# First-layer queries and keys in six weight tiles instead of eight, the gates' input columns as separate fp32 products

## The chip, the cores and the metric

The kernel runs on one core of one Trainium2 chip. The metric is the time of one launch on the device, in microseconds; the median of three runs is shown, and one further execution was recorded by the hardware profiler. PE (TensorE) multiplies, DVE (VectorE) and ACT (ScalarE) work on tiles, POOL (GpSimd) does a little elementwise work, and SP (SyncE) issues most of the DMAs.

## The reference, cut to what matters

One step of a two-layer decoder over 1024 prompt tokens and 8 sample tokens (1032 columns in all), width 1024. Only the first layer's input projection is touched:

```python
h = rmsnorm(x, norm_mix_pre[l])
q, k, v, r, glr, qm = split_cols(h @ w_in_a[a], IN_A_SIZES)   # 384, 384, 768, 768, 16, 256 columns
q = q.reshape(B, L, 4, 96) * (96 ** -0.5)
k = k.reshape(B, L, 4, 96)
g = jax.nn.log_sigmoid((glr @ w_gate_up[a] + b_gate[a]).astype(jnp.float32)) / 16
o, S = gla_recurrence(q, k, v, g, gla_state[a])               # gated linear attention, 4 heads
o_mem = mem_attend(qm, mem_k[l], mem_v[l])                    # attention into 256 memory tokens
```

`glr` are the 16 gate columns: a second, small product makes the 384 gates from them. The rest of the first layer (output projection, MLP) and the whole second layer are the same before and after.

## The kernel before, in words

Everything is kept transposed: features on the 128 partitions, tokens along the free axis, in three chunks of 384, 384 and 264 columns (`CH`). The 1024 input features are eight slices `k` of 128.

A large product is done in three passes of a reduced format: x and each weight are split into a rounded part and a remainder, x into `xh` and `xl`, a weight into `wh` and `wl`. `proj` (L241) multiplies one weight tile of 128 output columns with one chunk: for each of the eight slices `wh*xh`, `wh*xl`, `wl*xh`, 24 products that add up in one accumulator bank. A weight tile therefore costs 72 products over the three chunks. `wload` (L212) fetches a weight tile (512 KB), ACT rounds it to `wh` (L153), DVE makes `wl` (L154).

The norm's factor r is one number per token. It is not put on x but on the result: each accumulator is read out ("evicted") by DVE, which multiplies by r. r itself comes from squares on ACT, sums on DVE, a product with `ones` on PE (L199) and a few steps on ACT and DVE.

The first layer's stages are, in the order of the program:

1. `load_x` (L1003): 12 pieces of x, four for each chunk, two slices each, go through seven load buffers `ld` (L985). ACT rounds each piece with the norm's gain to `xh` (L994), DVE makes `xl` (L995), ACT squares it (L181). A buffer can be loaded again when all its readers are done.
2. `in_qm` (L1159): two weight tiles, the queries for the memory attention.
3. The keys and values of the memory (`memkv`), woven in between the first two query tiles.
4. The memory attention: scores into `sA` (L382), softmax on DVE and ACT, transposes (L401), output (L409), eight times; then the same for the 8 sample tokens, which ends with the transposes L461. In between stand the products of the other six query and key tiles, which keep PE busy while the softmax runs, and `gates` (L1228).
5. The branch (L1401): gated linear attention in one of two forms, chosen by a flag from the gates; behind it everything else.

Queries and keys stand in `qk`, eight slots of 128 partitions of which a head uses 96, rows 0 to 95. A weight tile is one head: 96 columns, or 112 for the first one, where the 16 gate columns stand behind the head's and land in rows 96 to 111 of slot 0. Row 112 is 1.0 for the bias. So `gates` multiplies rows 96 to 127 of slot 0 (32 rows) with the gate weights `wg`, 17 rows filled up with zeros.

The accumulators of stages 1 to 3 are two banks `mm` and four `mx` (`pm0`, L1207), taken in turn by `mmps`. Instructions are put in order, engine by engine, by a scheduler with priorities; `late` and `tick` (L122) hold a product back until so many columns of other products have been put ahead of it. On every engine the order is then fixed: an instruction that waits holds up those behind it.

## Time and profile before

| | |
|---|---|
| median of three runs | 2275.08 us (2273.16 to 2279.07) |
| profiled execution, time | 2279.71 us |
| its span, first to last instruction | 2277.9 us |
| mean granted TensorE clock | 0.99 |
| branch of the gated attention (start of the first L1303) | 222.29 us |
| first product on PE | 11.96 us |

A row of the timeline gives the start, the length, the engine, the line, the operation with its tiles, how many instructions are merged, and in brackets the idle time of the engine ahead of it and what ended it. Products overlap, so the distance between two starts, not the length, is what one costs. A fp32 product that is not split counts as two records.

### The profile page before, as it was taken

How to read it: one execution, taken by the hardware profiler on the slowest of the kernel's cores; microseconds unless marked ns; L12 is line 12 of the kernel's file. 1: busy time of each engine (PE TensorE's matmuls, PEld its weight loads, DVE VectorE, ACT ScalarE, POOL GpSimd, SP SyncE). 2: the span in 40 equal slices, each digit the busy share in tenths (PEclk: the TensorE clock that was granted, in tenths of full speed). 3: DMA queues.
4: the chain of work that ended last, by engine and by line, in shares of the span. 5: the costliest groups of instructions: out<-in, count | busy, mean ns of one | idle time of the engine just before them, and what ended most of it. 6: DMA issues, size and time to landing. Idle time of an engine off the chain costs nothing. (4 is left out here: it accounts for less than half of the span.)

```text
span 2277.9 us, 40266 instructions
## 1 busy us (share of the span) xinstructions
PE 2210.1 (97%) x16340; PEld 2093.2 (92%) x16340; DVE 1508.5 (66%) x2788; ACT 1062.4 (47%) x2064; POOL 76.0 (3%) x78
## 2 busy tenths in 40 slices
PE   7999999999999999899999999999999999999997
PEld 6868999899999999899999878679999999999996
DVE  7543565767887777756559555645987777756547
ACT  6451544546654544333334355644754445333333
POOL 0000100000000000320000000200000000000000
PEclk9999999999999999999999999999999999999998
DMA  5412013544363448665324200413364445735422
GB/s 197 144 53 98 13 55 94 158 144 130 123 202 131 139 153 305 234 243 165 108 62 148 94 20 29 133 61 101 114 198 161 154 138 212 261 106 160 152 95 75
DMA packets 136261, 305.41 MB, mean 134 GB/s; under 512 B 11274, under 2 KB 65619, under 8 KB 135779
## 3 DMA queue, kind: packets, MB, share of 16 engines
q1 hardware_dynamic: 122962, 276.75, 36.9%
q0 software_dynamic: 3312, 13.30, 1.9%
q10 hardware_dynamic: 9792, 12.68, 1.5%
q8 instruction: 131, 2.15, 0.4%
q14 instruction: 64, 0.52, 0.1%
HBM read 215.25 MB, written 89.51 MB: 134 GB/s over the span
## 5 line engine op out<-in xcount | busy, mean ns | idle before, releaser
L153 ACT CAST wh<-ws 128x512 fp32r<-128x512 f32 (+1 forms) x264 | 190.2, 728 | 353.4 <-DVE ws L576 104.5
L245 PE MATMUL mm<-xh,wh 128*128 128x384 f32 (+3 forms) x904 | 295.0, 327 | 15.3 <-ACT wh L153 12.0
L723 PE MATMUL mx<-xf,wh 128*128 128x258 f32 x1048 | 297.7, 284 | 0.0
L154 DVE TENSOR_TENSOR wl<-ws,wh 128x512 fp32r<-128x512 f32 (+1 forms) x264 | 216.4, 826 | 121.1 <-ACT wh L153 120.1
L724 PE MATMUL mx<-xf,wh 128*128 128x258 f32 x1048 | 296.0, 282 | 0.0
L725 PE MATMUL mx<-xf,wl 128*128 128x258 f32 x1048 | 295.1, 282 | 0.0
L247 PE MATMUL mm<-xh,wl 128*128 128x384 f32 (+3 forms) x904 | 292.9, 324 | 0.2 <-DVE wl L154 0.2
L246 PE MATMUL mm<-xl,wh 128*128 128x384 f32 (+3 forms) x904 | 292.3, 323 | 0.0
L153 ACT CAST wh<-wr 128x1024 fp32r<-128x1024 f32 x98 | 103.0, 1051 | 326.3 <-PE sx L889 307.3
L154 DVE TENSOR_TENSOR wl<-wr,wh 128x1024 fp32r<-128x1024 f32 x98 | 122.3, 1248 | 172.9 <-ACT wh L153 172.9
L889 PE MATMUL mx<-sa,wh 128*128 128x258 f32 x784 | 221.2, 282 | 6.1 <-DVE sa L154 6.1
L888 PE MATMUL mx<-sa,wh 128*128 128x258 f32 x784 | 222.3, 284 | 0.8 <-DVE aw L565 0.7
L890 PE MATMUL mx<-sa,wl 128*128 128x258 f32 x784 | 221.0, 282 | 0.0
L724 PEld LDWEIGHTS mx<-xf,wh 128*128 128x128 f32 x1048 | 198.0, 189 | 0.4
L723 PEld LDWEIGHTS mx<-xf,wh 128*128 128x128 f32 x1048 | 197.6, 189 | 0.4
L725 PEld LDWEIGHTS mx<-xf,wl 128*128 128x128 f32 x1048 | 197.9, 189 | 0.0
L245 PEld LDWEIGHTS mm<-xh,wh 128*128 128x128 f32 (+1 forms) x904 | 167.1, 185 | 25.6 <-ACT wh L153 12.5
L247 PEld LDWEIGHTS mm<-xh,wl 128*128 128x128 f32 (+1 forms) x904 | 166.7, 184 | 8.8 <-issue 6.5
L246 PEld LDWEIGHTS mm<-xl,wh 128*128 128x128 f32 (+1 forms) x904 | 167.2, 185 | 7.7 <-issue 5.8
L889 PEld LDWEIGHTS mx<-sa,wh 128*128 128x128 f32 x784 | 148.9, 190 | 6.3 <-DVE sa L154 6.3
L888 PEld LDWEIGHTS mx<-sa,wh 128*128 128x128 f32 x784 | 147.9, 189 | 1.9 <-DVE aw L565 1.1
L890 PEld LDWEIGHTS mx<-sa,wl 128*128 128x128 f32 x784 | 148.6, 189 | 0.0
(539 smaller groups left out, 5764.5 us busy)
## 6 DMA issues: line engine op xcount, KB each, us to landing
ra<-awd SPq DMA_DIRECT2D x98, 516.0 KB, 4.1
ws<-in_w_up SPq DMA_DIRECT2D x64, 512.0 KB, 5.2
wr<-in_w_downb SPq DMA_DIRECT2D x56, 512.0 KB, 5.4
awd<-aw SPq DMA_DIRECT2D x26, 1032.0 KB, 6.8
awd<-am SPq DMA_DIRECT2D x28, 774.0 KB, 8.4
ws<-in_w_in_a SPq DMA_DIRECT2D x22, 512.0 KB, 3.5
xd<-f ACTq DMA_DIRECT2D x24, 384.0 KB, 4.8
ws<-in_w_out SPq DMA_DIRECT2D x16, 512.0 KB, 3.5
```

The source lines that it names most:

```text
L153: nc.scalar.copy(hi, src)
L154: (eng or nc.vector).tensor_tensor(lo, src, f32(hi), ALU.subtract)
L245: nc.tensor.matmul(ps[:M, :n], wh[:, k, :M], xh[:, k, :], start=(k == 0), stop=False)
L246: nc.tensor.matmul(ps[:M, :n], wh[:, k, :M], xl[:, k, :], start=False, stop=False)
L247: mm = nc.tensor.matmul(ps[:M, :n], wl[:, k, :M], xh[:, k, :], start=False, stop=(k == KT - 1))
L723: nc.tensor.matmul(ps, wh(k), xh, start=(k == 0), stop=False)
L724: nc.tensor.matmul(ps, wh(k), xl, start=False, stop=False)
L725: mm = nc.tensor.matmul(ps, wl(k), xh, start=False, stop=(k == n - 1))
L888: nc.tensor.matmul(ps, wh[:, q, ms], h, start=(jj == 0 and q == 0), stop=False)
L889: nc.tensor.matmul(ps, wh[:, q, ms], lo, start=False, stop=False)
L890: mm = nc.tensor.matmul(ps, wl[:, q, ms], h, start=False, stop=end)
```

## The change

The 384 query columns are laid into three full weight tiles of 128, and so are the keys: six tiles instead of eight. `PACK` says for each tile which columns belong to which head and to which rows of its slot they go, so every accumulator is evicted in two pieces:

```diff
+GR = 128
+PACK = [[(0, 96, 0, 0), (96, 128, 1, 64)], [(0, 64, 1, 0), (64, 128, 2, 0)], [(0, 96, 3, 0), (96, 128, 2, 64)]]
 ...
             def qk_units(m):
-                w = wload(wA, A["w_in_a"][WQK[m]])
+                w = wload(wA, A["w_in_a"][m])
+                slots_ = (QIDX, KIDX)[m // 3]
                 for c in range(3):
 ...
-                    M = 112 if m == 0 else 96
                     ps = mmps()
-                    proj(ps, w, hl, n, M)
-                    if m in QIDX:
-                        STT(qk[:96, m, c0 : c0 + n], ps[:96, :n], DK ** -0.5, r[:96], ALU.mult, ALU.mult)
-                        if m == 0:
-                            TT(qk[96:112, 0, c0 : c0 + n], ps[96:112, :n], r[96:112], ALU.mult)
-                    else:
-                        TT(qk[:96, m, c0 : c0 + n], ps[:96, :n], r[:96], ALU.mult)
+                    proj(ps, w, hl, n)
+                    for a, b, h, o in PACK[m % 3]:
+                        dst = qk[o : o + b - a, slots_[h], c0 : c0 + n]
+                        if m < 3:
+                            STT(dst, ps[a:b, :n], DK ** -0.5, r[a:b], ALU.mult, ALU.mult)
+                        else:
+                            TT(dst, ps[a:b, :n], r[a:b], ALU.mult)
 ...
-                for m in range(2, 8):
+                for m in range(2, 6):
                     in_qk(m)
```

The gate columns become a product of their own, in fp32, from the raw pieces of x while they lie in their load buffers. The weight has 32 columns (one empty, the 16 gates, 15 empty) for each of the eight slices. Slice k goes to the column group 32 * (k % 4) of the array, so the accumulator `mg` holds four partial sums, each of two slices, in four groups of 32 rows. They are added up in the gates' second product, since `wg` now holds the gate weights four times, once for each group; row 0 is the bias, against a row of ones. ACT copies the sums out, DVE multiplies them by r later:

```diff
+            def gate_weights():
+                with tc.high_priority(4 * WPRI):
+                    nc.scalar.dma_start(wlow, A["w_glow"])
+                    TT(wlow, wlow, gains[:, G_MIXPRE, :].unsqueeze(2).to_broadcast([P, KT, 32]), ALU.mult)
+
+            def gate_sums(c, j, xs):
+                n = CH[c][1]
+                if j == 0:
+                    gsum[c] = extra[0].tile([P, 512], F32, tag="mg", name=nm("mg"), bufs=1)[:, :n]
+                row = Row()
+                for k in (2 * j, 2 * j + 1):
+                    q = 32 * (k % (GR // 32))
+                    mm = nc.tensor.matmul(gsum[c][q : q + 32], wlow[:, k, :], xs[:, k % 2, :],
+                                          start=(k < GR // 32), stop=(k >= KT - GR // 32))
+                    row(mm)
+                    if c:
+                        late.append([mm.ins, (c - 1) * 3 * KT * 384 + 6 * 384 * (j + 1)])
+                if j < 3:
+                    return
+                b0 = CH[c][0] // P
+                for i in range(b0, min(b0 + 3, NB)):
+                    nc.scalar.copy(gin[:GR, i // 2, i % 2, :], gsum[c][:GR, (i - b0) * P : (i - b0 + 1) * P])
+                if c == 2:
+                    nc.scalar.copy(gdec, gsum[c][:GR, 2 * P : n])
+
+            def gate_inputs():
+                for i in range(NB):
+                    g, r = gin[:GR, i // 2, i % 2, :], X[i // 3][1]
+                    TT(g, g, r[:GR, i % 3 * P : i % 3 * P + P], ALU.mult)
+                TT(vtok[:GR, 3, :NDEC], gdec, X[2][1][:GR, 2 * P :], ALU.mult)
+                nc.gpsimd.memset(gin[0:1], 1.0)
+                nc.gpsimd.memset(vtok[0:1, 3, :NDEC], 1.0)
 ...
-            with tc.tile_pool(name="pm0", bufs=4, space=PSUM, reuse_waits="tile") as pm0:
-                set_extra(pm0, 4)
+            with tc.tile_pool(name="pm0", bufs=3, space=PSUM, reuse_waits="tile") as pm0:
+                set_extra(pm0, 3)
                 w0 = []
-                load_x(lambda: w0.append(wload(wA, A["w_in_a"][20], 4 * WPRI)))
+                gate_weights()
+                load_x(lambda: w0.append(wload(wA, A["w_in_a"][18], 4 * WPRI)), gate_sums)
 ...
-                nc.tensor.matmul(zps[:, :384], qk[96:128, 0, i * P : i * P + P], wg[96:128, :],
+                nc.tensor.matmul(zps[:, :384].rearrange("p (a b) -> p a b", a=2), gin[:GR, i // 2, i % 2, :], wg,
                                  start=True, stop=True)
```

`load_split` calls `gate_sums` for every piece behind its load, so a load buffer has one reader more. `mg` is a single bank, taken from the `mx` tiles, of which three are left; the next chunk's sums need it copied out first. In the first memory query tile `proj` now calls `tick` after every slice (`fine`), so that `late` can place the gate products between them.

How the instructions move is shown at three places. On PE, from the start of the program, first before, then now (`mm` is the first memory query accumulator, `mg` the gate sums, `ld` a piece of x, and `vtok` holds the gate weight here):

```order
L245 MATMUL mm_274<-xh_126,wh_139 128x384
L246 MATMUL mm_274<-xl_127,wh_139 128x384
L247 MATMUL mm_274<-xh_126,wl_140 128x384
L245 MATMUL mm_274<-xh_126,wh_139 128x384
L246 MATMUL mm_274<-xl_127,wh_139 128x384
```

```order
L1136 MATMUL mg_132<-ld_130,vtok 32x384 x2
L1136 MATMUL mg_132<-ld_139,vtok 32x384 x2
L246 MATMUL mm_311<-xh_127,wh_143 128x384
L247 MATMUL mm_311<-xl_128,wh_143 128x384
L1136 MATMUL mg_132<-ld_153,vtok 32x384 x2
L248 MATMUL mm_311<-xh_127,wl_144 128x384
L246 MATMUL mm_311<-xh_127,wh_143 128x384
L247 MATMUL mm_311<-xl_128,wh_143 128x384
L1136 MATMUL mg_132<-ld_161,vtok 32x384 x2
```

The first two pairs of gate products, for the first and the second piece of x, stand ahead of the first memory query product, and the other ten pairs between products of the first two memory query tiles' chunks.

On ACT at the same time, first before, then now (`xh` is the rounded x, `tq` a square):

```order
L994 ACTIVATE xh_126<-ld_147,gains 128x384 x2
L994 ACTIVATE xh_126<-ld_153,gains 128x384 x2
L181 ACTIVATE tq_164<-ld_147 128x768
L994 ACTIVATE xh_178<-ld_181,gains 128x384 x2
L994 ACTIVATE xh_178<-ld_187,gains 128x384 x2
```

```order
L1000 ACTIVATE xh_127<-ld_153,gains 128x384 x2
L1145 COPY vtok<-mg_132 128x128 x3
L1000 ACTIVATE xh_127<-ld_161,gains 128x384 x2
L182 ACTIVATE tq_177<-ld_153 128x768
L1000 ACTIVATE xh_191<-ld_194,gains 128x384 x2
```

The copies of the first chunk's gate sums, which need all four pairs of that chunk, stand ahead of the rounding of the chunk's last piece.

On DVE where the first memory attention's softmax runs, first before, then now (`sm` are maxima and sums, `p` the probabilities, `qk` the queries and keys):

```order
L394 TENSOR_TENSOR p_967<-p_967,sm_980 128x1024
L1236 SCALAR_TENSOR_TENSOR vtok<-sx_1244,vtok 128x384
L387 TENSOR_REDUCE sm_1007<-sA_1001 128x4
L1111 TENSOR_TENSOR qk<-mm_1435,r_128 96x384
L393 RECIPROCAL sm_1013<-sm_1006 128x4
```

```order
L398 TENSOR_TENSOR p_1017<-p_1017,sm_1030 128x1024
L1155 TENSOR_TENSOR vtok<-vtok,r_251 128x8
L391 TENSOR_REDUCE sm_1057<-sA_1051 128x4
L1282 SCALAR_TENSOR_TENSOR vtok<-sx_1294,vtok 128x384
L1115 SCALAR_TENSOR_TENSOR qk<-mm_1485,r_129 96x384
L1115 SCALAR_TENSOR_TENSOR qk<-mm_1485,r_129 32x384
```

The eviction of a query tile is now two instructions ahead of the softmax's next step, and the scaling of the eight sample columns of the gate sums (L1155) stands in front of the second maximum.

## The prediction

> **What bounds the kernel now.** First the page's busy lines, then the busy time of the engines in stretches cut at the stages that the change touches.

> ```profile
> span 2277.9 us, 40266 instructions
> PE 2210.1 (97%) x16340; PEld 2093.2 (92%) x16340; DVE 1508.5 (66%) x2788; ACT 1062.4 (47%) x2064; POOL 76.0 (3%) x78
> 12.00:31.83 19.83, 15.12 (x67) 12.92 (x67) 17.02 (x30) 16.44 (x31) 0.00 (x0) 1.00 0.87 278
> 31.83:46.77 14.94, 14.94 (x85) 14.61 (x85) 13.16 (x24) 10.44 (x21) 0.00 (x0) 0.89 0.34 107
> 46.77:98.00 51.23, 49.30 (x356) 46.81 (x354) 32.19 (x57) 18.14 (x27) 0.00 (x0) 1.00 0.46 141
> 98.00:190.12 92.12, 90.08 (x504) 58.27 (x504) 40.96 (x61) 42.76 (x112) 0.00 (x0) 0.98 0.27 86
> 190.12:222.29 32.17, 32.17 (x208) 30.37 (x207) 9.39 (x18) 2.10 (x2) 1.80 (x1) 1.00 0.16 51
> 222.29:2277.90 2055.61, 2008.45 (x15131) 1930.20 (x15129) 1393.48 (x2595) 968.38 (x1869) 72.66 (x71) 0.99 0.41 135
> ```

> The columns after the length are the busy times of PE, PEld, DVE, ACT and POOL, then the granted clock, the DMA share and GB/s. PE is the bound from 31.83 us on. Only the first 32 us are shared: there PE idles 19.83 - 15.12 = 4.7 us, while VectorE and ScalarE are at 17.0 and 16.4 of 19.8 and DMA at 0.87. At 222.29 the gated-attention branch begins; behind it all engines keep their order of instructions, so I take those 2055.6 us as unchanged. The sum concerns the first 222.3 us.

> **Six tiles for eight.** A tile is 72 products. The bare stretch before the branch prices one, and the start of the program shows full columns and, until 17.9 us, half clock:

> ```profile
> 199.70 0.34 PE L245 MATMUL mm<-xh,wh 128*96 128x384 f32 x1
> 199.88 0.34 PE L246 MATMUL mm<-xl,wh 128*96 128x384 f32 x1
> ...
> 211.00 0.34 PE L245 MATMUL mm<-xh,wh 128*96 128x384 f32 x1
> ...
> 17.22 0.52 PE L247 MATMUL mm<-xh,wl 128*128 128x384 f32 x1
> 17.54 0.52 PE L245 MATMUL mm<-xh,wh 128*128 128x384 f32 x1
> ...
> 18.29 0.34 PE L245 MATMUL mm<-xh,wh 128*128 128x384 f32 x1
> 18.46 0.33 PE L246 MATMUL mm<-xl,wh 128*128 128x384 f32 x1
> ```

> 211.00 - 199.70 = 11.3 us, so two tiles are **-22.6 us**. 128 columns instead of 96 do not lengthen a product: both start 0.17 to 0.18 us apart at full clock (0.32 at half). This counts only if the tiles did not hide something. They stand among the memory attentions (98 to 190 us), whose softmax PE must otherwise wait for. By the two orders, 226 of the 432 products stand ahead of the last transposes of the decode attention before, and 236 of 288 now: the cover stays, and the bare stretch of 206 products shrinks to 52. At its end the attention mask must be ready:

> ```profile
> 189.88 0.30 PE L461 MATMUL sT<-ident,od 32*128 32x32 f32 x2
> ...
> 193.50 0.22 DVE L1284 TENSOR_SCALAR causal<-triu 128x128 uint8<-128x128 f32 x1
> ```

> It follows those transposes by 3.8 us, and 52 products last 28 x 0.175 + 24 x 0.12 = 7.8 us, so nothing new is late. Two weight loads with their splits go too, off the path.

> Each projection is now evicted in two pieces instead of one (36 VectorE instructions for 27). One costs the same whatever its rows:

> ```profile
> L1109 DVE TENSOR_TENSOR qk<-mx,r 16x384 f32<-16x384 f32 x1 | 0.6, 565 | 0.0
> L1107 DVE SCALAR_TENSOR_TENSOR qk<-mx,r 96x384 f32<-96x384 f32 x1 | 0.6, 554 | 0.3 <-PE mx L247 0.3
> ```

> VectorE is at 41 of 92 us there, but the second piece stands ahead of a softmax step some six times: between 0 and 6 x 0.55 = 3.3 us. PE idles only 2.0 us in that stretch, so I take **+0.5**. Where the first attention's probabilities have been scaled, VectorE also waits for a store to land before it scales the eight sample columns:

> ```profile
> 102.84 1.23 DVE L394 TENSOR_TENSOR p<-p,sm 128x1024 f32<-128x1024 f32 x1
> ...
> 103.48 0.49 ACT L1233 ACTIVATE vtok<-sx 128x384 f32<-128x384 f32 x1 [0.88 <-DMA mvd<-vtok]
> ```

> The store lands at about 103.4, VectorE arrives at 104.1: 0. Were that cover gone, the next maximum and the next scores behind it would slip by as much as the store is late.

> **The gates' second product** reads 128 rows instead of 32. The nearest full-height fp32 product is that with ones:

> ```profile
> 107.60 0.91 PE L1231 MATMUL sx<-vtok,qk 32*128 32x384 f32 x2
> ...
> 108.44 0.41 PE L247 MATMUL mm<-xh,wl 128*96 128x384 f32 x1
> ...
> 24.95 0.81 PE L199 MATMUL sf<-r,ones 128*128 128x384 f32 x2
> ...
> 25.65 0.39 PE L246 MATMUL mx<-xl,wh 128*128 128x264 f32 x1
> ```

> Its slot is 0.70 instead of 0.84 us: nine times -0.14 is **-1.2**, or 0 if the height costs. The nine scalings by r (up to 0.28 us each, 2.5 together, ahead of a weight's split) fall where VectorE has 32.2 of 51.2 us, the two POOL fills of one row where POOL shows 0.00, the larger gate-weight load where DMA is at 0.46: 0, and 2.5 if VectorE's room is gone.

> **The gates' first product** moves to the start of the program: 24 fp32 products of 32 columns, two per piece of x, on two column groups side by side. Such a pair is not in the trace; the nearest is the attention's output product, four products on two 64-column halves:

> ```profile
> 108.78 1.08 PE L409 MATMUL sf<-pt,vtok 128*64 128x256 f32 x8
> ...
> 109.79 0.42 PE L245 MATMUL mm<-xh,wh 128*96 128x384 f32 x1
> 110.05 0.34 PE L246 MATMUL mm<-xl,wh 128*96 128x384 f32 x1
> ```

> From 108.44 to 110.05 is 1.61 us, less two projections 1.26. Two rounds at 0.70 x 256/384 = 0.47 make 0.94, and 0.32 is left for changing the shape of the array; one after the other the four would take 1.87. A pair is then 0.70 + 0.32 = 1.02 us at 384 wide, 0.80 at 264. The first pair runs before PE's first weight has come. Eleven are left: 7 x 1.02 + 4 x 0.80 - 0.32 (two neighbours) = 10.0, and +1.4 for two whose streaming doubles at half clock: 11.4 us. If the halves did not overlap it would be about 18.

> [...]

> What covers them:

> ```profile
> 11.96 0.69 PE L245 MATMUL mm<-xh,wh 128*128 128x384 f32 x1 [11.96 <-ACT wh L153]
> ...
> 12.84 1.12 ACT L994 ACTIVATE xh<-ld,gains 128x384 fp32r<-128x384 f32 x2 [0.93 <-DMA ld<-in_xT]
> ...
> 28.48 0.29 PE L245 MATMUL mx<-xh,wh 128*128 128x264 f32 x1
> ...
> 31.83 0.69 PE L245 MATMUL mx<-xh,wh 128*128 128x384 f32 x1 [3.06 <-ACT wh L153]
> ...
> 14.60 2.12 ACT L994 ACTIVATE xh<-ld,gains 128x384 fp32r<-128x384 f32 x4
> ...
> 23.00 0.38 SPq L985 DMA_DIRECT2D ld<-in_xT  x1
> ...
> 225.75 1.12 ACT L1328 ACTIVATE tq<-gL,sm 96x128 f32<-96x128 f32 x4
> ```

> Now PE starts its projections behind the second piece of x, which lands at 12.84 (0.35 later with 128 KB more in flight): 13.2. Up to the second weight stand 11.4 us of pairs and about 11.4 of projections and sums (48 x 0.175 + 12 x 0.125 + 0.70 + 0.8 for the first few at half clock): 36.0. ScalarE could delay that too: its three copies of the gate sums (0.28 each) wait for the fourth pair, and everything behind them waits: the rounding of x, the squares that free x's load buffers on SP's queue, and the cast of the second weight, which I reach at about 35. Before, the second weight's first product stood at 31.83, with four products of the third chunk still behind it that now stand ahead: 31.83 + 0.5, so 3.7 us late. Some comes back:

> ```profile
> 32.00:34.00 2.00, 2.00 (x8) 2.00 (x9) 2.00 (x4) 1.87 (x3) 0.00 (x0) 0.50 0.00 0
> 35.23 0.34 PE L247 MATMUL mx<-xh,wl 128*128 128x384 f32 x1
> ```

> After the idle 3.06 us PE ran at half clock until 35.2: ten products in 3.4 us that take 1.7 at full clock. Without that idle time this goes: -1.7. [...]

> Last, one accumulator goes from the mx tiles to the gates, five for six. The second chunk of the first query tile now needs the one that waits for the third chunk's r:

> ```profile
> 44.72 0.61 PE L199 MATMUL sf<-r,ones 128*128 128x264 f32 x2
> ...
> 49.97 0.43 DVE L1166 SCALAR_TENSOR_TENSOR qm<-mx,r 128x264 f32<-128x264 f32 x1
> ```

> That takes 5.7 us from the sum to the eviction, and PE has 0.4 + 24 x 0.175 = 4.6 of work in between: +1.1; VectorE, at 13.2 of 14.9 us here and started later, may add as much again: +2.0. The start costs 3.7 - 1.7 + 2.0 = **+4.0 us**, between 0 (all inside the old 4.7 us) and 10 (the 11.4 us with nothing of them covered but the clock).

> **Sum:** -22.6 + 0.5 - 1.2 + 4.0 = **-19.3 us**. The profiled execution took 2279.7 us (span 2277.9), which is 4.6 above the median shown; the same difference on the median 2275.1 gives 2255.8.

> **The rivals.**
> - *The start is hidden.* The pairs fall into waits for x and the half clock goes: 0 or -1.7. For: 4.7 us idle, DMA at 0.87. Against: pairs behind 13 us stand between products. -22.6 + 0.5 - 1.2 - 0.5 = -23.8: 2251.3.
> - *The start costs twice as much.* The copies hold ScalarE, so x's buffers come free late and the weights with them. For: SP issued its last x load only at 23.00, behind such a square. Against: the second weight now stands ahead of the last x piece. With +10: -13.3: 2261.8.
> - *The tiles hid latency.* If half of the bare stretch's gain comes back as waits in the attentions, 11.3 us are left: -8.0: 2267. Against: 236 covering products for 226.
> - *Slower: lockstep at the start.* Each of the eleven pairs waits for its piece, and ScalarE, behind its copies, delays the next piece; each turn costs the 3.06 us that PE waited once. 11 x 3.06 = 33.7 against -23.3: +10.4, 2285.5; it decides from 2.1 us a pair. Against: from 14.60 ScalarE rounds piece after piece without a wait, so they land ahead of it.
> - *The change does not do what it says*, for instance a third piece per tile: the order shows 134 rows fewer on PE, so no chance.

> **How the numbers follow.** My forecast 0.63 (start +1 to +8: 2252.8 to 2259.8), hidden 0.15, twice as much 0.14, latency 0.05, lockstep 0.03. The range 2249 to 2265 holds the first three with 2 us of spread of the runs; what it leaves out is the last two and edges, under 0.2. A change under 0.3% (6.8 us) can hardly be told from none: faster 0.93 (the first three and some of the fourth), same 0.04, slower 0.03.

> **What would show it.** In the new profile: the branch at about 203 us instead of 222.3, and what follows at 2055 us; 72 products per tile at 11.3 us; between the decode attention's last transposes and the branch 8 us; pairs of 1.0 us; the second weight's first product at about 36 us with no idle time ahead of it and the clock at 1.00; a wait of 1 to 2 us for an accumulator near 54 us. Wrong would be: idle time of several us beside each pair, PE waiting on softmax between 80 and 170 us, or the part behind the branch longer by more than 3 us.

## The result, and the profile after

| | before | after |
|---|---|---|
| median, 8 runs each | 2275.89 us (2273.16 to 2281.05) | 2261.07 us (2248.70 to 2265.92) |
| profiled execution, time and span | 2279.71, 2277.9 us | 2265.92, 2264.1 us |
| second weight's first product on PE | 31.83 us | 34.64 us |
| start of the branch | 222.29 us | 202.86 us |
| from the branch to the end of the span | 2055.6 us | 2061.2 us |

The ratio is 0.9926 with an interval of 0.9905 to 0.9947: faster by 0.5 to 0.95%, 14.8 us between the medians. Between the two profiled executions it is 13.8 us, and they show at once how that comes about: the front part gained 19.4 us, the part behind the branch lost 5.6. The busy lines of the changed kernel's page:

```profile
span 2264.1 us, 40118 instructions
PE 2195.5 (97%) x16244; PEld 2078.0 (92%) x16244; DVE 1513.7 (67%) x2803; ACT 1061.7 (47%) x2071; POOL 79.0 (3%) x80
```

PE has 14.6 us less to do, and its share is the same 97%. Its busy time in stretches cut at its own marks (columns as in the prediction):

```profile
12.48:34.64 22.16, 22.16 (x107) 12.27 (x107) 15.83 (x26) 16.16 (x35) 0.00 (x0) 1.00 0.65 215
34.64:98.00 63.36, 60.73 (x429) 59.28 (x428) 46.97 (x91) 27.81 (x50) 1.50 (x2) 1.00 0.44 142
98.00:190.00 92.00, 87.37 (x510) 63.00 (x509) 47.82 (x72) 44.29 (x115) 0.09 (x1) 0.98 0.29 90
190.00:202.86 12.86, 12.03 (x73) 9.95 (x71) 5.52 (x13) 0.00 (x0) 1.82 (x1) 1.00 0.27 92
202.86:2264.10 2061.24, 2011.74 (x15131) 1933.31 (x15129) 1395.85 (x2596) 969.25 (x1869) 74.62 (x71) 0.99 0.41 135
```

In the first line of stretches PE has no idle time left: the pairs of gate products stand where it waited for x and for the second weight. In the second it idles 2.6 us and POOL, which showed 0.00 there, does something for 1.50 us; in the third it idles 4.6 us, where the kernel before idled 2.0 (98 to 190.12). The last line holds as many products as before, 15131, so its 5.6 us must lie in waits and in the clock.

A pair of gate products, alone and beside the next one, in the timeline of PE:

```profile
19.65 0.34 PE L248 MATMUL mm<-xh,wl 128*128 128x384 f32 x1
19.92 0.84 PE L1136 MATMUL mg<-ld,vtok 128*32 128x384 f32 x4
20.69 0.45 PE L246 MATMUL mm<-xh,wh 128*128 128x384 f32 x1
20.97 0.34 PE L247 MATMUL mm<-xl,wh 128*128 128x384 f32 x1
...
28.03 0.65 PE L1136 MATMUL mg<-ld,vtok 128*32 128x264 f32 x8
28.61 0.44 PE L246 MATMUL mx<-xh,wh 128*128 128x384 f32 x1
```

From 19.65 to 20.97 is 1.32 us; less two projections at 0.175 the pair costs 0.97. Two neighbouring pairs on all four column groups take 0.58 us at 264 columns (28.03 to 28.61), no more than one pair (29.87 to 30.44, 0.57).

**Behind the branch.** Laying the products of the two profiles beside each other one by one shows the offset between them grow at few places. The largest, 4.1 us, is where the arm of the branch that was taken ends and PE jumps over the other arm. First before, then after:

```profile
278.76 0.39 PE L245 MATMUL mm<-xh,wh 128*128 128x264 f32 x1 [3.04 <-issue]
278.98 0.28 PE L246 MATMUL mm<-xl,wh 128*128 128x264 f32 x1
...
281.65 0.29 PE L247 MATMUL mm<-xh,wl 128*128 128x264 f32 x1
```

```profile
259.26 0.39 PE L246 MATMUL mm<-xh,wh 128*128 128x264 f32 x1 [2.94 <-issue]
259.48 0.28 PE L247 MATMUL mm<-xl,wh 128*128 128x264 f32 x1
...
260.20 0.36 PE L247 MATMUL mm<-xl,wh 128*128 128x264 f32 x1
262.37 0.59 PE L248 MATMUL mm<-xh,wl 128*128 128x264 f32 x1 [1.81 <-issue]
262.76 0.42 PE L246 MATMUL mm<-xh,wh 128*128 128x264 f32 x1
262.98 0.42 PE L247 MATMUL mm<-xl,wh 128*128 128x264 f32 x1
```

"issue" means that nothing in the trace holds PE. Before, all 24 products of the chunk follow one wait of 3 us, without another; now a second wait comes 8 products behind the first, and the products behind it start 0.22 us apart instead of 0.12: half clock (0.50 granted from 261 to 267 us). The other places are small: half clock between 525 and 545 us (+1.1), +0.7 between 275 and 400, +0.8 between 900 and 1000, and -1 in the rest.

**POOL's queue.** What POOL did in the second stretch, before and after:

```profile
1.36 0.74 POOL L1668 DMA_DIRECT2D out_swa_ks<-in_swa_k_nat  x1 [0.91 <-POOLq L1875]
2.09 0.60 POOL L1669 DMA_DIRECT2D out_swa_vs<-in_swa_v_nat  x1
```

```profile
1.36 0.74 POOL L1715 DMA_DIRECT2D out_swa_ks<-in_swa_k_nat  x1 [0.91 <-POOLq L1925]
61.76 0.95 POOL L1156 MEMSET vtok<- 1x1024 f32 x1 [59.66 <-DVE vtok L1154]
62.66 0.60 POOL L1716 DMA_DIRECT2D out_swa_vs<-in_swa_v_nat  x1
```

The fill of the gates' row of ones waits for the last scaling of the gate inputs, and behind it on POOL's queue stands a copy of the second layer's value cache to the output (1016 KB). It ran in the first microseconds; now it starts at 62.7, among the loads of the memory weights. The cast of the third of them in the timeline of ScalarE, then the DMA issues of 62 to 75 us (KB each, median us to landing) and PE's waits of 36 to 190 us (us in total, times, longest), all of the changed kernel:

```profile
72.79 1.05 ACT L154 CAST wh<-ws 128x1024 fp32r<-128x1024 f32 x1 [8.30 <-DMA ws<-in_w_mem]
```

```profile
ws<-in_w_mem SPq DMA_DIRECT2D x2, 512.0 KB, 9.8
out_swa_vs<-in_swa_v_nat POOLq DMA_DIRECT2D x1, 1016.0 KB, 9.9
```

```profile
PE sf L1064 <- DVE vtok L1056: 2.7, 1, 2.7
PE sx L1064 <- DVE vtok L1056: 2.5, 1, 2.5
```

The weights land 9.8 us after their issue, as late as the copy, and PE waits twice for the memory values that are made with them. Before, it waited for them once:

```profile
PE sf L1057 <- DVE vtok L1049: 1.9, 1, 1.9
```

Whether the place of the code and the displaced copy are causes is what the experiments are for.

### The profile page after: what moved, and what is told of

Same layout as the page of the kernel before. It is cut to its first block, busy times and chain, and to the rows that moved or that the text cites. A ratio compares the mean times of both kernels' runs of the same rounds, so it can differ in the third digit from the quotient of the medians.

```text
span 2264.1 us, 40118 instructions
## 1 busy us (share of the span) xinstructions
PE 2195.5 (97%) x16244; PEld 2078.0 (92%) x16244; DVE 1513.7 (67%) x2803; ACT 1061.7 (47%) x2071; POOL 79.0 (3%) x80
## 3 DMA queue, kind: packets, MB, share of 16 engines
q0 software_dynamic: 3312, 13.30, 1.9%
q8 instruction: 130, 2.13, 0.4%
## 5 line engine op out<-in xcount | busy, mean ns | idle before, releaser
L246 PE MATMUL mm<-xh,wh 128*128 128x384 f32 (+1 forms) x864 | 282.7, 328 | 3.0 <-issue 2.9
L248 PE MATMUL mm<-xh,wl 128*128 128x384 f32 (+1 forms) x864 | 281.3, 326 | 1.8 <-issue 1.8
L247 PE MATMUL mm<-xl,wh 128*128 128x384 f32 (+1 forms) x864 | 278.7, 323 | 0.0
L246 PEld LDWEIGHTS mm<-xh,wh 128*128 128x128 f32 x864 | 163.9, 190 | 13.4 <-issue 10.1
L248 PEld LDWEIGHTS mm<-xh,wl 128*128 128x128 f32 x864 | 163.6, 189 | 10.1 <-issue 8.1
L247 PEld LDWEIGHTS mm<-xl,wh 128*128 128x128 f32 x864 | 164.0, 190 | 6.0 <-issue 4.8
```

What stands on the lines that cost most here:

```text
L246: nc.tensor.matmul(ps[:M, :n], wh[:, k, :M], xh[:, k, :], start=(k == 0), stop=False)
L247: nc.tensor.matmul(ps[:M, :n], wh[:, k, :M], xl[:, k, :], start=False, stop=False)
L248: mm = nc.tensor.matmul(ps[:M, :n], wl[:, k, :M], xh[:, k, :], start=False, stop=(k == KT - 1))
```

## The experiments

Several profiles of one code give an idea of what repeats. Each row is one profile, times in us. A fold is POOL's multiplication of a weight of 128 x 1024 by the norm's gain (L238 to L240), of which twelve stand behind 850 us:

| code | second weight's first product | branch | the 15.7 us behind the end of the branch | PE idle near 950 us, longest fold |
|---|---|---|---|---|
| before | 31.83 | 222.29 | 11.64 | 6.1, 9.97 |
| before, 32 dead products | 31.64 | 221.52 | 14.21 | 8.0, 9.88 |
| before, 164 dead products | 30.80 | 219.92 | 16.55 | 6.8, 9.90 |
| after | 34.64 | 202.86 | 15.74 | 7.5, 13.03 |
| after, again | 35.54 | 204.46 | 15.85 | 7.7, 13.30 |
| after, 20 dead products | 33.56 | 203.73 | 11.83 | 1.6, 3.66 |
| after, 6 dead products | 34.65 | 200.57 | 17.18 | 2.1, 3.45 |

The fourth column is the time from the first product behind the jump to the product that stands 15.74 us behind it in the changed kernel. The dead products stand in the arm that is not taken, so up to the branch the rows of one code should differ by the execution alone: the branch stands at 221.2 on the mean before and 202.9 after, 18.3 us apart.

**Again, and with padding.** The edit in `after_pad` (10 products in each of two tiles; `pad6` 3, `before_pad` 16, `before_pad164` 82):

```diff
                     with cmp.Else():
+                        for dead in (mmps(), mmps()):
+                            for _ in range(10):
+                                nc.tensor.matmul(dead[:, :264], W[0][0][:, 0, :], X[2][0][0][:, 0, :], start=True, stop=True)
                         in_v(range(3), W, part=slice(0, NB))()
```

> The changed kernel once more, as control and to see what repeats from one execution to the next. In its first profile PE waited 2.94 us and then, 13 products later, 1.81 us more behind the branch (262.37 us), and ran at half clock until 266 us; a second stretch at half clock stood at 528 to 534 us. Theory 'place of the code': the wait of 1.8 us and the half clock behind it come back at the same 13 products, the stretch at 528 us may or may not. Rival 'chance': the 1.8 us wait is gone or stands elsewhere. Branch at 202.9 us within 0.5 by both; median 2258 to 2264.

> The changed kernel with 20 matrix products put into the arm of the branch that is not taken, so that only the place of the code behind the branch moves (by 40 instructions, if weight load and product are one each). Place of the code: the first wait of about 3 us stays, the second one (1.81 us) and the half clock behind it are gone, so what lies behind the branch falls by about 4.2 us, from 2061.2 to 2057, and the median by 3 to 5. Chance, or a delay that comes from the data (weights, DMA): nothing changes by the pad, the second wait stands where it stood, same median.

> The kernel before with 32 such products in the arm that is not taken. The change took 96 products (by the records of the trace) off PE ahead of the end of the branch; if PE's instructions come in blocks of 128 or 256 and a product is two, moving the code by 64 gives the old kernel the place that the changed one has. Place of the code: a second wait of 1 to 2.5 us appears some 5 to 20 products behind the first in the old kernel, with half clock behind it in most cases: 2 to 5 us slower. Chance, or a delay that comes from the change's data: nothing changes, 2276.

The ratios are to the kernel before, run beside them on the same chip. `after_again`: 2262.16 us (ratio 0.9922, 0.9902 to 0.9942), 17.3 under the kernel before; the second wait is back, 2.0 us, again behind the 8th product (the expectation counted 13, wrongly), and the branch at 204.46 lies outside the expected 202.9 plus or minus 0.5. `after_pad`: 2256.46 us (0.9904, 0.9885 to 0.9923), only the first wait, 11.83 us instead of 15.8. The medians are 5.7 us apart, but the intervals overlap, and in the profile PE also idled 6 us less near 950 us; it is the stretch behind the jump that tells, not the total. `before_pad`: 2279.03 us (0.9999, 0.9984 to 1.0015), no second wait that the profile names. Two of three came as the theory had it. The next two runs test it further.

> The changed kernel with 6 products in the arm that is not taken. Place of the code: PE's break moves with the padding, so the second wait comes 6 products earlier, behind the 7th product instead of the 13th after the branch, and is longer by these products' time, 1.8 to 2.0 + 6 x 0.12 = 2.5 to 2.7 us. Rival 'any padding takes the second wait away': no second wait.

> The kernel before with 164 products in the arm that is not taken. In the built programs PE's code is 34584 instructions of 64 bytes long for the kernel before and 34401 for the changed one, and what lies behind the branch is the same in both, so the end of the branch stands 183 instructions earlier in the changed kernel. Its second wait came behind 8 products, and behind 2 with 6 products of padding; 32 products of padding in the kernel before brought none. Blocks of 512 instructions (32 KB) agree with all of these, blocks of 128 or 256 do not agree with the last. With 164 products (329 instructions less one) the old kernel's end of the branch stands at the same place in a block of 512 as the changed kernel's. Place of the code: a second wait of 1.3 to 2.0 us appears 8 products behind the first in the old kernel. Rival 'it belongs to the change': only the first wait, as in both other profiles of the old code.

Each of the two was run once: `pad6` 2252.84 us, `before_pad164` 2284.68 us, against medians of 2280.63 and 2280.10 of the kernel before beside them. `pad6` is among the fastest of the changed kernel's runs in spite of its second wait, with an early branch (200.57) and little idle time near 950 us (2.1), so again the total does not decide. The timeline of PE in `pad6`, `before_pad164` and `before_pad`, each behind the jump:

```profile
257.02 0.59 PE L246 MATMUL mm<-xh,wh 128*128 128x264 f32 x1 [2.99 <-issue]
257.40 0.42 PE L247 MATMUL mm<-xl,wh 128*128 128x264 f32 x1
260.53 0.59 PE L248 MATMUL mm<-xh,wl 128*128 128x264 f32 x1 [2.70 <-issue]
```

```profile
275.95 0.39 PE L245 MATMUL mm<-xh,wh 128*128 128x264 f32 x1 [2.61 <-issue]
...
276.90 0.28 PE L246 MATMUL mm<-xl,wh 128*128 128x264 f32 x1
279.44 0.38 PE L247 MATMUL mm<-xh,wl 128*128 128x264 f32 x1 [2.26 <-issue]
```

```profile
277.66 0.59 PE L245 MATMUL mm<-xh,wh 128*128 128x264 f32 x1 [2.71 <-issue]
...
280.02 0.42 PE L246 MATMUL mm<-xl,wh 128*128 128x264 f32 x1
280.25 0.42 PE L247 MATMUL mm<-xh,wl 128*128 128x264 f32 x1
280.59 0.38 PE L245 MATMUL mm<-xh,wh 128*128 128x264 f32 x1
```

With 6 dead products the break comes 6 products earlier, behind the 2nd, and the wait is 2.70 us, as expected. With 164 the kernel before gets the changed kernel's second wait, behind the 8th product. So it does not belong to the change's data: it goes with where the code lies. The last fence mends the reading of `before_pad`. Its products stand 0.22 us apart (half clock), but between the 12th and the next are 0.34: the break is there, and at half clock the 12 products had filled nearly all the time up to it: the next came 2.93 us after the first product, where it came after 3.11 in `after`, 3.51 in `pad6` and 3.49 in `before_pad164`. By the place of the code in blocks of 256 instructions, two per product (the page counts as many weight loads as products, 16244 each), the break belongs behind the 8th, 2nd, 8th and 12th product in these four, which is where it stands; my step to blocks of 512 came from overlooking that row. The row of the code's own DMA queue on the changed kernel's page fits:

```profile
q8 instruction: 130, 2.13, 0.4%
```

130 packets of together 2.13 MB are 16.4 KB each, 256 of the 64-byte instructions of the built programs. One of them moved between 259.8 and 260.3 us in the changed kernel, ahead of the second wait, and one between 279.0 and 279.5 before, where no second wait came. That PE waited for such a packet is not shown; what the runs show is that the wait goes with the place of the code.

What the second wait costs: the five profiles with code at such a place (also `vs_late` and `swa_late`, below, 15.58 and 16.62 us) and `pad6` took 15.6 to 17.2 us in that stretch. The others took 11.6 to 14.2, the lower end where no half clock fell into it (`before`, `after_pad`, `best`), the upper where 6.8 us of it did (`before_pad`, `nogate`). That is 1.4 to 5.5 us, 4.1 between the two profiles.

**The gates' first products left out**, with the copies of their sums; the gates come from the bias alone.

```diff
             def gate_sums(c, j, xs):
+                return
...
+                nc.gpsimd.memset(gin[:GR], 0.0)
+                nc.gpsimd.memset(gdec, 0.0)
                 load_x(lambda: w0.append(wload(wA, A["w_in_a"][18], 4 * WPRI)), gate_sums)
```

> The changed kernel without the gates' 24 fp32 products at the start and without the copies of their sums (the gate inputs are set to 0 instead, so the gates come from the bias alone); the mx tiles stay three. By the steps of the forecast the start then costs only the accumulator: second weight's first product at 34.64 less about 9 to 11 us of pairs, but not before the second weight is ready, which was 31.8 in the kernel before: so 31 to 32 us and a branch at about 200 us (2 to 3 us earlier). Rival 'the pairs are paid in full': branch 9 us or more earlier, near 194. Rival 'the pairs are hidden': branch within 0.7 us of 202.9. Place of the code: 96 instructions fewer ahead of the end of the branch, so no second wait there, and what lies behind it falls to about 2057.

2250.21 us. The second weight's first product stood at 30.82, behind an idle 2.06 us, 3.8 us earlier than the 34.6 of the four profiles; the branch at 197.63, 5.3 earlier than their mean, between the expected 2 to 3 and the rival's 9. So the pairs and the copies of their sums cost 3.8 us at the second weight. The other 1.5 us are not theirs for certain: from the second weight to the branch this one profile had 3.4 us of half clock, and the four of the changed kernel between 0 and 6.8. No second wait stood behind the branch, as the place of the code asks for.

**The packing alone undone**: eight tiles of 96 columns, the gates' products as in the change.

```diff
-                    proj(ps, w, hl, n)
-                    for a, b, h, o in PACK[m % 3]:
...
+                    proj(ps, w, hl, n, 96)
+                    if m in QIDX:
+                        STT(qk[:96, m, c0 : c0 + n], ps[:96, :n], DK ** -0.5, r[:96], ALU.mult, ALU.mult)
+                    else:
+                        TT(qk[:96, m, c0 : c0 + n], ps[:96, :n], r[:96], ALU.mult)
...
+        for h in hd:
+            cols += [h, np.zeros((D, 32), f)]
```

> The packing alone undone: eight tiles of 96 columns, the gates' products as in the changed kernel. Tiles worth 11.3 us each: the branch comes 22.6 us later than in the changed kernel (mean of three profiles 203.7), at 226.3, less 0.5 if the second evictions cost. Rival 'the tiles hid latency': 8 to 18 us later only. Behind the branch: 96 instructions more or fewer change the place of the code, so no second wait there is expected.

One run, 2284.89 us, against 2280.63 (2278.02 to 2287.61) of the kernel before beside it: no gain without the packing. The branch stood at 223.69, 20.8 us behind the mean of the changed kernel's (19.2 to 23.1 behind the single ones); 22.6 lies inside. From the second weight's first product to the branch it took 190.6 us, against 168.3 with six tiles on the mean: 22.3.

**The displaced copy.** First the one copy put behind the fill at 195 us, then both copies, then both in the kernel before.

```diff
-                nc.gpsimd.dma_start(O["swa_vs"][:, : WIN - 1, :], A["swa_v_nat"][:, 1:, :])
+                cp = nc.gpsimd.dma_start(O["swa_vs"][:, : WIN - 1, :], A["swa_v_nat"][:, 1:, :])
+                tc.add_manual_dep(cp.ins, fill[0], NOSYNC, reason="copy behind the fill")
...
-                nc.gpsimd.memset(AT1, 0.0)
+                fill.append(nc.gpsimd.memset(AT1, 0.0).ins.name)
```

> The changed kernel with one instruction of POOL's queue moved: the copy of the value cache to the output (1016 KB) stands behind the fill at 195 us instead of behind the fill of the gates' constant row. In the changed kernel that fill waits for the scaling of the gate inputs, so the copy starts at 62.7 us instead of 2.1 us, in the middle of the loads of the memory weights, and the cast of the third of them waits until 72.8 us. Theory 'displaced copy': without it those weights land some 3 us earlier, the two waits of PE for the memory values (5.3, 4.6 and 5.8 us in three profiles) fall to 1 to 3 us together, and the branch comes 2 to 4 us earlier than the mean of the three, 203.7: 200 to 202 us. Rival 'VectorE is the cause' (nine scalings and two-piece evictions ahead of the memory values): waits and branch as they were, 203 to 204.5. Start as in the changed kernel by both: second weight's first product at 33.5 to 35.5.

> The changed kernel with both copies of the caches to the outputs (2 x 1016 KB) behind the fill at 195 us. Besides what the displaced copy costs, this takes the other copy out of the first 12 us, where DMA is at 0.8. If the pieces of x come later for it, the second pair of gate products starts at 10 to 11 us instead of 11.8 to 13.1, the branch at 198 to 201 us, and the run is 3 to 6 us faster than the changed kernel. If only the latency of the loads counts, start as before and the branch as in the run with one copy moved.

> The kernel before with both copies of the caches behind the fill ahead of the branch, as in the run swa_late of the changed kernel. If the copies delay x at the start whatever the rest does, PE's first product, 11.96 us before, comes at 8 to 9.5 us, the second weight's first product (31.83) some 2 to 4 us earlier, and the run is 2 to 5 us faster than the kernel before. Then the packing with its fp32 products is worth, with the copies out of both, the difference to swa_late: branch 192.94 there; 22.6 less the price of the pairs (3 to 5 us), so a branch at 211 to 213 here. Rival 'the gap at the start is the weight's cast': first product at 11.5 or later and nothing gained.

The same three views of `vs_late`:

```profile
66.69 1.05 ACT L155 CAST wh<-ws 128x1024 fp32r<-128x1024 f32 x1 [2.44 <-DMA ws<-in_w_mem]
```

```profile
ws<-in_w_mem SPq DMA_DIRECT2D x3, 512.0 KB, 4.0
```

```profile
PE sf L1065 <- DVE vtok L1057: 2.9, 1, 2.9
```

The weights land after 4.0 us instead of 9.8, and the first of the two waits, 2.4 to 3.7 us in all four profiles of the changed kernel's front, is gone. In `unpacked` and `nogate`, where the copy is displaced as well, that first wait is 1.9 and 0.6 us, so what the copy costs depends on how much time the memory values have. The second wait stays, at the upper end of the expected 1 to 3. The branch came at 200.11, 2.8 us before the mean of the four, the median is 2257.03 us (0.9886, 0.9866 to 0.9907). The wait and the landing settle the mechanism; the 2.8 us come from one profile, within the spread of the branch in the four (3.9), and one of the four (200.57) was nearly as early.

`swa_late`: 2251.64 us (0.9864, 0.9846 to 0.9882), second pair at 7.95 us instead of 12.5, branch at 192.94: 10 us earlier than the change, more than expected. The copies hold up x. The kernel before gains from it too, at the start: `before_late` 2274.65 us (0.998, 0.9962 to 0.9998), first product at 8.14, second weight's at 25.91, branch at 217.68, which misses the expected 211 to 213. The clock accounts for the miss: between the second weight and the branch this profile had 10.2 us of half clock, which cost up to 5.1, and that of `swa_late` had none; 217.7 less 5.1 is 212.6. So the 24.7 us between the two branches are no price of the packing. At the second weight, ahead of that half clock, `swa_late` stands at 30.36, 4.5 us behind `before_late`: with the copies out of both, the gates' products still cost their 3 to 5 us.

**Two versions beyond the change.** First both copies late, 20 dead products and the gates' products in groups of four; then also the DMAs of the folded weights on POOL's own queue.

```diff
-                for k in (2 * j, 2 * j + 1):
+                held[j] = xs
+                if j % 2 == 0:
+                    return
+                for k in (2 * j, 2 * j + 1, 2 * j - 2, 2 * j - 1):
...
-        nc.sync.dma_start(ws, src)
+        nc.gpsimd.dma_start(ws, src)
...
-        nc.sync.dma_start(wfd[i], ws)
+        nc.gpsimd.dma_start(wfd[i], ws)
```

> The changed kernel with both copies late, 20 products of padding, and the gates' first products in six groups of four (four column groups side by side) instead of twelve pairs. In the changed kernel two pairs that stand side by side took 0.58 us together at 264 columns, and one alone 0.57: so a group of four costs about what a pair does, 1.0 us at 384, and some three to four pairs' time goes: the branch at 189 to 191 us against 192.94 in swa_late, no second wait behind it (1.26 there), 4 to 7 us faster than swa_late in all. Rival 'the groups of four stream one after the other': branch as in swa_late or later.

> As late_quad_pad, with the loads and stores of the weights that POOL folds (L238, L240) on POOL's own queue instead of SP's. In the profiles one fold takes 10 to 13 us instead of 2.5 where it falls on a run of VectorE instructions without a gap, its store holds SP's queue, the activations' loads stand behind it, and PE idles 3 to 8 us near 950 us; where no fold is stretched (two profiles) PE does not idle. Theory 'store ahead on SP's queue': with its own queue the idle time near 950 goes even where a fold is stretched, runs gather at the lower end: 2 to 6 us under late_quad_pad. Rival 'the folds themselves or DMA's share set it': idle time stays, same time; POOL's slower issue of its DMAs could cost.

`late_quad_pad`: 2247.78 us (0.9845, 0.9817 to 0.9873), branch at 191.12 and 3.9 us less than `swa_late` by the medians, each just outside what was expected; the two ran on different chips, and their intervals overlap. A group of four costs what a pair did, 0.79 us from its start to the next product's, where the pair at 19.92 took 0.77:

```profile
14.85 0.85 PE L1140 MATMUL mg<-ld,vtok 128*32 128x384 f32 x8
15.64 0.45 PE L247 MATMUL mm<-xh,wh 128*128 128x384 f32 x1
```

`best`: 2240.71 us (0.9822, 0.9794 to 0.9850), 7.1 us under `late_quad_pad`, more than the expected 2 to 6, and some 20 under the changed kernel by the medians of different chips. Its five runs lie within 3.4 us (2238.94 to 2242.30) where those of the changed kernel spread over 17. What the theory started from is the changed kernel's timeline near 950 us, rows of SP's queue, POOL, VectorE and PE in order of time, with the fold of a weight that elsewhere took 1.9 to 2.8 us:

```profile
929.77 0.42 SPq L851 DMA_DIRECT2D wr<-in_w_downb  x1
...
931.75 13.03 POOL L239 TENSOR_TENSOR wf<-wf,gains 128x1024 f32<-128x1024 f32 x1 [9.16 <-DMA wf<-in_w_in_b]
...
941.79 1.22 DVE L155 TENSOR_TENSOR sa<-ra,sa 128x1032 fp32r<-128x1032 f32 x1
942.94 1.41 DVE L557 TENSOR_TENSOR acc<-mx,acc 128x258 f32<-128x258 f32 x4
...
944.80 0.33 SPq L240 DMA_DIRECT2D wfd<-wf  x1
945.18 0.42 SPq L845 DMA_DIRECT2D ra<-awd  x1
...
989.90 0.55 PE L892 MATMUL mx<-sa,wh 128*128 128x258 f32 x1 [5.91 <-DVE acc L560]
```

SP issues nothing for 15 us: the fold's store is the next on its queue, and the load of activations stands behind it. In `best` a fold was stretched even further (timeline of POOL), and PE did not idle at all (stretch of 860 to 1000 us):

```profile
901.19 14.59 POOL L240 TENSOR_TENSOR wf<-wf,gains 128x1024 f32<-128x1024 f32 x1 [5.76 <-DMA wf<-in_w_kv]
```

```profile
860.00:1000.00 140.00, 140.00 (x1172) 140.00 (x1171) 96.57 (x94) 52.57 (x58) 46.35 (x31) 1.00 0.73 256
```

That is what the theory asked for. The stretched fold is not the whole of it, though: PE idled 3.8 us between 860 and 1000 us in `late_quad_pad` with no fold over 3.0 us, 5.3 in `swa_late` with none over 4.0, and only 3.0 in `nogate` with one of 13.1. What held PE in the first two was not followed, and how the held load reaches PE's wait 45 us later was not traced step by step.

## Why the prediction was right, and where not

- **Six tiles, -22.6**: right. 22.3 us by `unpacked` from the second weight on. The cover in the attentions held: PE's waits for softmax (L405) were 1.3 us in the changed kernel, 0.9 (L401) before.
- **From the second weight to the branch** the stretch can be split. On the mean it took 189.8 us in the three profiles before and 168.3 in the four after, 21.5 less. Without PE's idle time and half of the time at half clock, 183.0 to 183.9 are left before and 158.2 to 159.0 after: by this estimate 24.9 us less work, near the 22.6 and 1.2 of the prediction. Idle time took 3.4 us back (7.7 for 4.3), and half clock nothing either way (4.3 us of it on both means).
- **Second evictions, +0.5, and the gates' second product, -1.2**: not measured alone. What is left in the same way in `unpacked`, 182.4, lies 0.6 to 1.6 us under the kernel before, so the -1.2 is possible and "0 if the height costs" unlikely.
- **The pairs, 1.0 us each and the second weight 3.7 late**: right in size, with a slip in the count. A pair cost 0.97 us; the second weight's first product stood at 31.4 on the mean of three profiles before and at 34.6 on that of four after, 3.2 late, where 36.0 was forecast. The prediction adds 0.5 us for four products of the third chunk "that now stand ahead". The traces show 16 of the 24 ahead of the second weight before and 12 after: the four moved behind it. With the sign put right the steps give 36.0 - 31.3 = 4.7 us, where 34.6 - 30.9 = 3.7 was measured. No run shows the 0.32 us for changing the shape of the array by itself: it is an estimate, what was left over of 1.26. Of the pair's 0.97 the gaps at its two ends take 0.2: the starts stand 0.27 and 0.28 us apart there instead of 0.175.
- **The half clock, -1.7**: right at its place and lost again. PE did not idle from 12.48 us on, two projections side by side stood 0.17 to 0.18 us apart from 18.76 on, and the half clock behind the second weight was gone, 1.00 granted where 0.50 was (twelve products stand in those 3.4 us before, not ten; the 1.7 holds). But one of the three profiles before (`before_pad164`, 2.3 us of idle time) had none there either, and in two of the four after, half clock set in at 77 us, at the new wait for the memory values.
- **The accumulator, +2.0**: wrong. PE did not idle at all between 46 and 60 us in the changed kernel.
- **"The two POOL fills of one row where POOL shows 0.00 ...: 0"**: the step that failed. The fills are free, 0.95 and 0.09 us on an idle POOL; what is queued behind the first one is not. A copy was moved past 60 us of POOL's queue into the loads of the memory weights, and a new wait of 2.4 to 3.7 us came of it. It has about the size of the accumulator's 2.0, so the sum of the front came out right, -19.4 in the profiled pair and -18.3 on the means. That these two errors cancel is luck.
- **"I take those 2055.6 us as unchanged"**: wrong by 5.6 us in the profiled pair, and "the part behind the branch longer by more than 3 us" was one of the prediction's own signs of being wrong. The order is the same on every engine, but the code lies at another place: 4.1 us at the end of the branch, which dead code puts into the old kernel and takes out of the new one. This is the main part of what separates -19.3 from the measured -14.8. The rest is no more than two measurements of the same two kernels differ: the second gave -17.3.
- **The rivals**: hidden pairs and lockstep are excluded by the 3.2 us and by PE without idle time from 12.48 to 34.64; latency hidden by the tiles by `unpacked`. The median is almost the 2261.8 of "the start costs twice as much", but by another way: the second weight was 3.2 us late, not some 10, and the loss lies behind the branch.

## What to carry to other kernels

Behind a new fill that waited on POOL's queue a copy slipped from 2.09 to 62.66 us: for a new instruction that waits, list what stands behind it on its queue, bulk copies with no reader above all, and give such copies a place where the DMA engines are idle. Behind the jump, the place of the code cost 1.4 to 5.5 us, and edits upstream changed it; dead instructions in the arm that is not taken test for that, and here 20 products took the second wait out of the changed kernel and 164 put it into the one before. A part of the program with the same order of instructions took 2055.6 us in one kernel and 2061.2 in the other, so compare two traces product by product before calling a part unchanged.
